# A two-block transformer on one core: depthwise convolutions summed in PSUM, modulation products paced along the feed-forward, merge gates taking turns with taps

## The chip, the cores and the metric

The kernel runs on one core of one Trainium2 chip. The core has five engines that work side by side, each through its own list of instructions in a fixed order: TensorE for matmuls (PE in the profile, PEld its weight loads), VectorE (DVE), ScalarE (ACT), GpSimd (POOL) and SyncE (SP), which here issues every DMA. Matmuls write PSUM, used here as eight banks of [128, 512] float32; everything else lies in SBUF. The metric is the device time of one execution in microseconds.

## The reference

There are 512 tokens of width 1024, all in float32. Block 1 takes a normed input through one wide projection into three branches, and then through a convolutional feed-forward:

```
u = causal_dwconv(h @ w_up, dw_w) + dw_b          # 3 taps a channel
a, v = split(u);  y = (silu(a) * v) @ w_down      # 2 x 2816 channels

a, gate = split(u_conv);  z = a * sigmoid(gate)   # conformer branch, 512 channels
z = causal_dwconv(z, dw_w) + dw_b                 # 31 taps a channel
z = silu(layer_norm(z)) @ w_proj

x = x + (g_a * y_attn + g_b * y_conv) @ w_out     # g = sigmoid(merge gates)
```

`y_attn` is an attention with compressed, selected and windowed keys, 8 heads. Block 2 has two attention layers whose norms are modulated by `mod = silu(c) @ ada_w[layer] + ada_b[layer]`, 3072 numbers for each layer, which depend on the conditioning vector `c` alone.

## The kernel before, in words

Activations lie transposed, features on partitions and the 512 tokens along the free dimension, so that a tile is [128, 512]. A float32 matmul is made of three (`mm3`, L123 to L125): each operand is split into a rounded high part and a low part. So `gemm` of eight K tiles loads weights in two pieces of 512 columns (SP), splits each (ACT at L109, mostly POOL at L110) and runs 24 matmuls into one PSUM bank. That bank is read once by DVE: the evacuation, a multiplication by the row of reciprocal norms (L575 for a merge gate, L666 for an up projection).

The PSUM banks are four pools: `pg` (2) for gemms, `ps` (2) for scores and, from the branches on, for every other gemm (`wide_bank`), `pt` (3) for transposes and `po` (1) for a head's values.

The program is written for a scheduler that orders each engine's list by its own estimate of readiness, with earlier written code first; buffers come from pools in turn. `tc.issue_after(ins)` makes the instructions of a block, as far as they are on `ins`'s engine, stand behind `ins` in that engine's list; it adds no wait, and other engines (the DMAs on SP too) aren't bound by it. What comes out is a fixed list for each engine, with semaphores.

The stages that matter here, with their times in the profile:

- Attention of block 1 (104 to 245 us). For each head and branch: scores (PE, L501), maximum with bias (DVE, L505), exponent (ACT, L507), normalisation (POOL, L509), transposes (PE, L253) split by ACT and DVE (L257, L258), values (PE, L263). `group_compressed` (L448, L449) makes the compressed branch once for each group of four heads. In this stage `conv_input` (L407, L410) makes the four channel tiles `zs` of the conformer branch, and `conv_start` (ACT, L421) the first tap of each.
- Taps and merge gates (to 323 us). A tap is one DVE instruction on a channel tile, `conv[c] = zs[c][:, t:t+512] * w + conv[c]` (L586, 120 of them for 4 tiles), in SBUF. The loop writes both gates of a feature tile and then 16 or 20 taps, for seven of eight tiles. Nothing but data binds them, so the scheduler places taps in attention too.
- The mean over channels (PE, L601 and L602), the squares, a chain of small DVE instructions for the reciprocal root (L156 to L170), its broadcast (PE, L176), norm and SiLU; then the branch projections (`branch`) and the output projection.
- Feed-forward (434 to 814 us). `up(j)`: two gemms, each with its evacuation (L666), first tap (ACT, L668), two taps (DVE, L670), then SiLU and product (POOL, L673). 13 ups, half the down projections, 9 ups, the rest of the down projections. `modulation(n)` is written behind each: a row of 48 columns takes two products with a sum (DVE, L652; operands from HBM, 256 KB each) and an addition of the two sums and the bias (L654). Block 2 needs the results only at its first norm.

Of the kernel before, what the change touches and what calls it, by code (L numbers as in the profile page):

```python
# [43 lines left out]
def build(ctx, tc, I, out):  # L44
# [107 lines left out]
    def newton(x):  # L152
# [4 lines left out]
        # one step of the second order, three eighths of its result, and one of the third:  # L157
        # y * (15 - 10 x y^2 + 3 x^2 y^4) / 8
# [26 lines left out]
    class Squares:  # L185
        """Sums over features of the squares of [128, tokens] chunks."""
# [117 lines left out]
    # compressed keys and values  # L304
# [58 lines left out]
    # keys of the two token branches, queries  # L363
# [37 lines left out]
    # conformer branch: a * sigmoid(gate) = a / 2 * (1 + tanh(gate / 2)), causal depthwise conv, layer norm, silu  # L401
# [16 lines left out]
    def conv_start(c):  # L418
        z = zs[c]
        y = new("h")  # L420
        A.activation(y, z[:, 0:512], AF.Identity, bias=cv("cb", c), scale=cv("cw", c * 31))  # L421
        conv.append(y)

    # queries of one group and its compressed branch
# [67 lines left out]
    # token branches  # L492
# [48 lines left out]
    for h in range(8):  # L541
# [5 lines left out]
        if h == 0:  # L547
            PC.append(group_compressed(0, QG[0]))
            with after():
                conv_start(0)  # L550
# [6 lines left out]
        for b in range(2):  # L557
# [4 lines left out]
            if b == 0 and h in (1, 3, 5):  # L562
                with after():
                    conv_start((h + 1) // 2)
# [5 lines left out]
    def merge_gates(m):  # L570
        gts = []
        for b in range(2):
            ps = gemm(I["w_g"][2 * m + b], xg)
            t = new("m" if m < 4 else "h")
            V.tensor_mul(t, ps, R1)  # L575
            gts.append(t)
        return gts
# [3 lines left out]
    # causal depthwise convolution, layer norm over channels, silu  # L581
    for m in range(7):
        GM.append(merge_gates(m))
        for t in range(1 + 30 * m // 7, 1 + 30 * (m + 1) // 7):
            for c in range(4):
                V.scalar_tensor_tensor(conv[c], zs[c][:, t:t + 512], cv("cw", c * 31 + t), conv[c],  # L586
                                       op0=OP.mult, op1=OP.add)
    # branch projections with their gates, each twice its value
# [25 lines left out]
    GM += [merge_gates(m) for m in range(len(GM), KT)]  # L614
# [8 lines left out]
    # output projection, residual, norm 2  # L623
# [22 lines left out]
    def modulation(n):  # L646
        for l, m in mods[:n]:
            acc = new("s", (128, 16))[:, 0:2]
            for z in range(2):
                raw = new("b") if z else new("z", (128, 542))[:, 0:512]  # L650
                nc.sync.dma_start(raw, I["ada_t"][l, m, :, z * 512:(z + 1) * 512])
                V.tensor_tensor_reduce(out=raw, in0=raw, in1=CA[z], op0=OP.mult, op1=OP.add, scale=1.0,  # L652
                                       scalar=0.0, accum_out=acc[:, z:z + 1])
            V.scalar_tensor_tensor(MD[l][:, m:m + 1], acc[:, 0:1], acc[:, 1:2], cv("adab", 24 * l + m),  # L654
                                   op0=OP.add, op1=OP.add)
        del mods[:n]

    # one pair of up projections with its convolution and product
    def up(j):
        cs = []  # L660
        for b in range(2):
# [4 lines left out]
            V.tensor_mul(u[:, 2:514], ps, R2)  # L666
            t = new("p")
            A.activation(t, u[:, 0:512], AF.Identity, scale=cv("fw", 3 * m), bias=cv("fb", m))  # L668
            for i in (1, 2):
                V.scalar_tensor_tensor(t, u[:, i:i + 512], cv("fw", 3 * m + i), t, op0=OP.mult, op1=OP.add)  # L670
# [11 lines left out]
    for m in range(KT):  # L682
        ps = gemm(I["w_dn"][m][:, 0:11, :], ACTV, 11, wide_bank)
        V.tensor_add(X[m], X[m], ps)
# [4 lines left out]
    # a projection's last chunks go by halves of the tokens, so that the next norm overlaps with it  # L689
# [7 lines left out]
    for m in range(KT):  # L697
# [4 lines left out]
        V.tensor_add(X[m], X[m], ps)  # L702
# [23 lines left out]
    # final norm of block 1 and the first norm of block 2  # L726
    MOD = []
    for l in range(2):
# [533 lines left out]
```

## Time and profile before

| | |
|---|---|
| runs before | 1386.32, 1388.19, 1389.37 us; median 1388.19 |
| profiled execution | its time is told by its span alone: 1387.6 us from the first instruction to the last |
| matmuls, instructions in all | 6337, 19249 |
| mean granted PE clock | 0.971 |
| moved by DMA | 124.74 MB, mean 90 GB/s |

In the page's rows, "x" is a count; in a group of instructions the first number behind the bar is the time in which any of them ran, the second the mean of one in ns, the third the idle time of the engine just before them, with what ended it. A window's row begins with its bounds and length, then busy us (and count) of PE, PEld, DVE, ACT and POOL, the granted PE clock, the busy share of the DMA engines and GB/s. A timeline row begins with start and length in us; equal neighbours are merged, with their count at the end. Rows of one engine overlap a little: the step from one start to the next is shorter than a row's length.

### The profile page before, as it was taken

Reading aid. Unit: us, or ns where it says so; the run is one execution under the profiler, and the core shown is the slowest. Engines: PE = TensorE matmul, PEld = TensorE weight load, DVE = VectorE, ACT = ScalarE, POOL = GpSimd, SP = SyncE. Lnnn points to the kernel's source line nnn. Section 1 sums busy time; section 2 is a strip of 40 time slices with the busy share of each in tenths; the row PEclk is TensorE's granted clock in tenths of the full one; section 3 lists DMA queues with packets and bytes.
Section 4 is the critical chain, followed back from the end, with each engine's and each line's share of the span. In section 5 each row is a group of like instructions: output and inputs, shape, how many; then the busy total and the mean of one; then the engine's idle time right before and its main releaser. Section 6 shows DMA issues by size and latency. Waiting matters only on the chain.

```text
span 1387.6 us, 19249 instructions
## 1 busy us (share of the span) xinstructions
PE 1284.6 (93%) x6337; PEld 1052.3 (76%) x6337; DVE 983.8 (71%) x2117; ACT 690.1 (50%) x1467; POOL 707.2 (51%) x669
## 2 busy tenths in 40 slices
PE   6888889989999998889999997899999989999997
PEld 5777778767877876668888887777777778788886
DVE  7559999984545999972266548967688876666455
ACT  6735467325343323333344434367676745777554
POOL 4248475453643545466555526625444631676642
PEclk9999899999999998999999998999999999999998
DMA  7121101322344777724332320211111120212221
GB/s 222 46 84 56 37 31 56 114 78 82 107 122 129 234 226 228 229 85 137 99 92 78 109 80 26 77 39 35 50 62 39 39 62 28 64 54 62 61 77 61
DMA packets 71971, 124.74 MB, mean 90 GB/s; under 512 B 8256, under 2 KB 17344, under 8 KB 71872
## 3 DMA queue, kind: packets, MB, share of 16 engines
q1 hardware_dynamic: 71872, 123.52, 29.3%
q8 instruction: 50, 0.82, 0.3%
q14 instruction: 49, 0.40, 0.1%
HBM read 121.39 MB, written 2.10 MB: 89 GB/s over the span
## 4 chain that ended last, share of the span: by engine, by line
PE 59%; DVE 28%; ACT 5%; issue 4%; POOL 2%; DMA 2%; SPq 0%; DVEq 0%; ACTq 0%; POOLq 0%
PE pg L123 11%; PE pg L125 10%; PE pg L124 10%; DVE h L586 6%; PE po L263 5%; PE ps L123 4%; PE ps L124 4%; PE ps L125 4%; PE pt L253 3%; DVE p L670 3%; DVE b L652 2%; PE ps L869 2%; DVE z L652 2%; PE ps L1054 2%; PE ps L501 1%
## 5 line engine op out<-in xcount | busy, mean ns | idle before, releaser
L110 POOL TENSOR_TENSOR wl<-wr,wh 128x512 fp32r<-128x512 f32 (+2 forms) x215 | 296.7, 1383 | 319.2 <-ACT wh L109 256.9
L123 PE MATMUL pg<-h,wl 128*128 128x512 f32 x692 | 281.3, 407 | 8.5 <-DVE m L575 5.1
L124 PE MATMUL pg<-h,wh 128*128 128x512 f32 x692 | 277.3, 401 | 0.0
L125 PE MATMUL pg<-h,wh 128*128 128x512 f32 x692 | 276.5, 400 | 0.0
L109 ACT ACTIVATE wh<-wr 128x512 fp32r<-128x512 f32 (+2 forms) x215 | 131.7, 617 | 133.5 <-PE pg L125 74.5
L123 PEld LDWEIGHTS pg<-h,wl 128*128 128x128 f32 x692 | 131.6, 190 | 39.2 <-issue 11.6
L125 PEld LDWEIGHTS pg<-h,wh 128*128 128x128 f32 x692 | 131.6, 190 | 28.3
L124 PEld LDWEIGHTS pg<-h,wh 128*128 128x128 f32 x692 | 131.6, 190 | 27.3 <-issue 0.7
L110 POOL TENSOR_TENSOR m<-t,m 128x512 fp32r<-128x512 f32 (+1 forms) x67 | 93.3, 1392 | 78.7 <-ACT m L109 50.5
L670 DVE SCALAR_TENSOR_TENSOR p<-p,k,p 128x512 f32<-128x512 f32 x88 | 100.4, 1141 | 26.3 <-ACT p L668 25.4
L263 PE MATMUL po<-t,h 128*128 128x512 f32 (+3 forms) x384 | 111.5, 367 | 5.3 <-DVE t L258 2.7
L258 DVE TENSOR_TENSOR t<-pt,t 128x512 fp32r<-128x512 f32 (+1 forms) x160 | 97.3, 629 | 24.9 <-ACT t L257 24.3
L586 DVE SCALAR_TENSOR_TENSOR h<-z,k,h 128x512 f32<-128x512 f32 x120 | 113.4, 988 | 0.1
L257 ACT ACTIVATE t<-pt 128x512 fp32r<-128x512 f32 (+1 forms) x160 | 84.1, 551 | 26.3 <-PE pt L253 25.6
L253 PE MATMUL pt<-k,p 128*128 128x128 f32 x576 | 88.8, 276 | 1.7 <-POOL p L509 0.8
L263 PEld LDWEIGHTS po<-t,h 128*128 128x128 f32 x384 | 67.5, 192 | 27.2 <-ACT t L257 12.0
L253 PEld LDWEIGHTS pt<-k,p 128*128 128x128 f32 x576 | 70.1, 141 | 15.6 <-POOL p L876 3.5
L123 PE MATMUL ps<-h,wl 128*128 128x512 f32 x196 | 78.5, 401 | 1.8 <-ACT h L147 1.6
L124 PE MATMUL ps<-h,wh 128*128 128x512 f32 x196 | 78.0, 398 | 0.3 <-DVE h L148 0.2
L125 PE MATMUL ps<-h,wh 128*128 128x512 f32 x196 | 77.9, 397 | 0.0
L876 POOL TENSOR_SCALAR p<-p,s 128x512 f32<-128x512 f32 x64 | 44.9, 705 | 63.0 <-DVE s L875 62.4
L123 PE MATMUL ps<-h,m 128*128 128x512 f32 (+1 forms) x148 | 59.6, 402 | 15.5 <-DVE p L666 15.4
(367 smaller groups left out, 3003.5 us busy)
## 6 DMA issues: line engine op xcount, KB each, us to landing
b<-ada_t SPq DMA_DIRECT2D x48, 256.0 KB, 3.4
z<-ada_t SPq DMA_DIRECT2D x48, 256.0 KB, 3.4
t<-w_up SPq DMA_DIRECT2D x44, 256.0 KB, 2.9
wr<-w_up SPq DMA_DIRECT2D x44, 256.0 KB, 2.8
wr<-w_g SPq DMA_DIRECT2D x32, 256.0 KB, 2.6
t<-w_dn SPq DMA_DIRECT2D x23, 256.0 KB, 2.7
wr<-w_br SPq DMA_DIRECT2D x16, 256.0 KB, 2.7
wr<-w_gt SPq DMA_DIRECT2D x16, 256.0 KB, 2.7
```

The source lines that it names most:

```text
L109: A.activation(hi[:, :z], raw[:, :z], AF.Copy)
L110: eng.tensor_sub(lo[:, :z], raw[:, :z], f(hi[:, :z]))
L123: PE.matmul(ps, ll, rh, start=start and i == 0, stop=False)
L124: PE.matmul(ps, lh, rl, start=False, stop=False)
L125: PE.matmul(ps, lh, rh, start=False, stop=stop and i == n - 1)
L253: PE.transpose(ps[:, o:o + 128], src, ident)
L257: evac[:] = [A.activation(hi[:, :n], ps[:, :n], AF.Copy)]
L258: evac.append(V.tensor_sub(lo[:, :n], ps[:, :n], f(hi[:, :n])))
L263: PE.matmul(o[:, a:b], v, t[:, pa:pa + b - a], start=start and z == 0, stop=stop and z == 1)
L586: V.scalar_tensor_tensor(conv[c], zs[c][:, t:t + 512], cv("cw", c * 31 + t), conv[c], op0=OP.mult, op1=OP.add)
L652: V.tensor_tensor_reduce(out=raw, in0=raw, in1=CA[z], op0=OP.mult, op1=OP.add, scale=1.0, scalar=0.0, accum_out=acc[:, z:z + 1])
L670: V.scalar_tensor_tensor(t, u[:, i:i + 512], cv("fw", 3 * m + i), t, op0=OP.mult, op1=OP.add)
```

## The change

The convolution sums move to PSUM. A new `acc_bank` gives banks of `pt` and, every fourth time, of `po`. The four conformer sums hold three `pt` banks and the one `po` bank for all their taps; the last tap (t = 30) writes an SBUF tile. In `up`, the first two taps go to such a bank and the third reads it and writes SBUF. `conv_start` leaves the attention loop and is written behind it. Merge gates and taps take turns by single gates: one gate, then 8 or 9 taps that go round the four tiles, 14 times; the gates also use `wide_bank`. The modulation keeps the two sums of each column in a tile `MA` for each layer and adds them, with the bias, in two instructions a layer at the end; its products are put behind the last tap of the up, or the addition of the down projection, that is written before them. The tile `ss` of block 2 moves to another pool; the other lines of the difference are comments.

```diff
+    acount = [0]
+    def acc_bank():
+        acount[0] += 1
+        return new("po" if acount[0] % 4 == 0 else "pt")
...
     def conv_start(c):
-        z = zs[c]
-        y = new("h")
-        A.activation(y, z[:, 0:512], AF.Identity, bias=cv("cb", c), scale=cv("cw", c * 31))
+        y = acc_bank()
+        A.activation(y, zs[c][:, 0:512], AF.Identity, bias=cv("cb", c), scale=cv("cw", c * 31))
         conv.append(y)
+    def conv_tap(c, t):
+        if t == 30:
+            y, conv[c] = conv[c], new("h")
+        else:
+            y = conv[c]
+        return V.scalar_tensor_tensor(conv[c], zs[c][:, t:t + 512], cv("cw", c * 31 + t), y,
+                                      op0=OP.mult, op1=OP.add)
...
-            with after():
-                conv_start(0)
...
-            if b == 0 and h in (1, 3, 5):
-                with after():
-                    conv_start((h + 1) // 2)
...
+    def merge_gate(m, b):
+        ps = gemm(I["w_g"][2 * m + b], xg, bank=wide_bank)
+        t = new("m" if m < 4 else "h")
+        V.tensor_mul(t, ps, R1)
+        return t
+    for c in range(4):
+        conv_start(c)
+    taps = [(c, t) for t in range(1, 31) for c in range(4)]
     for m in range(7):
-        GM.append(merge_gates(m))
-        for t in range(1 + 30 * m // 7, 1 + 30 * (m + 1) // 7):
-            for c in range(4):
-                V.scalar_tensor_tensor(conv[c], zs[c][:, t:t + 512], cv("cw", c * 31 + t), conv[c],
-                                       op0=OP.mult, op1=OP.add)
+        GM.append([])
+        for b in range(2):
+            GM[m].append(merge_gate(m, b))
+            for c, t in taps[len(taps) * (2 * m + b) // 14:len(taps) * (2 * m + b + 1) // 14]:
+                conv_tap(c, t)
...
     def modulation(n):
-        for l, m in mods[:n]:
-            acc = new("s", (128, 16))[:, 0:2]
...
-            V.scalar_tensor_tensor(MD[l][:, m:m + 1], acc[:, 0:1], acc[:, 1:2], cv("adab", 24 * l + m),
-                                   op0=OP.add, op1=OP.add)
+        with tc.issue_after(getattr(paced[0], "ins", paced[0])):
+            for l, m in mods[:n]:
+                for z in range(2):
+                    raw = new("b") if z else new("z", (128, 542))[:, 0:512]
+                    nc.sync.dma_start(raw, I["ada_t"][l, m, :, z * 512:(z + 1) * 512])
+                    V.tensor_tensor_reduce(out=raw, in0=raw, in1=CA[z], op0=OP.mult, op1=OP.add, scale=1.0,
+                                           scalar=0.0, accum_out=MA[l][:, z, m:m + 1])
...
+            a = acc_bank()
             t = new("p")
-            A.activation(t, u[:, 0:512], AF.Identity, scale=cv("fw", 3 * m), bias=cv("fb", m))
-            for i in (1, 2):
-                V.scalar_tensor_tensor(t, u[:, i:i + 512], cv("fw", 3 * m + i), t, op0=OP.mult, op1=OP.add)
+            A.activation(a, u[:, 0:512], AF.Identity, scale=cv("fw", 3 * m), bias=cv("fb", m))
+            for i, dst in ((1, a), (2, t)):
+                paced[0] = V.scalar_tensor_tensor(dst, u[:, i:i + 512], cv("fw", 3 * m + i), a,
+                                                  op0=OP.mult, op1=OP.add)
...
-        V.tensor_add(X[m], X[m], ps)
+        paced[0] = V.tensor_add(X[m], X[m], ps)
...
     for l in range(2):
+        V.tensor_add(MD[l], MA[l][:, 0], MA[l][:, 1])
+        V.tensor_add(MD[l], MD[l], cv("adab", 24 * l, 24))
```

In the changed file the tap is L435, the gate's evacuation L582, the mean L610 and L611, the squares' sums L223 and L224, the broadcast L183, the up's evacuation and taps L675 and L680, the product L663 and DVE's split L152.

Three places of the orders follow. First DVE in attention, where the compressed branch of the second group is made (L410 and L417 are the same evacuation of `conv_input`, L448/L449 and L462/L463 the same sums of the group's scores). Before, with taps on the tiles of channels 0 and 1:

```order
L586 SCALAR_TENSOR_TENSOR h_1071<-z_1009,k_107,h_1071 128x512
L586 SCALAR_TENSOR_TENSOR h_1312<-z_1233,k_107,h_1312 128x512
L586 SCALAR_TENSOR_TENSOR h_1071<-z_1009,k_107,h_1071 128x512
L410 TENSOR_TENSOR p_1719<-pg_1694,r_284 128x512
L448 TENSOR_TENSOR p_1731<-ps_1732,b_1726 128x256
L586 SCALAR_TENSOR_TENSOR h_1312<-z_1233,k_107,h_1312 128x512
L449 TENSOR_TENSOR p_1731<-p_1731,ps_1732 128x256
```

After:

```order
L277 TENSOR_TENSOR h_1073<-po_1528,t_1636 64x512
L414 SCALAR_TENSOR_TENSOR p_1676<-pg_1651,r_284 128x512
L417 TENSOR_TENSOR p_1715<-pg_1690,r_284 128x512
L462 TENSOR_TENSOR p_1727<-ps_1728,b_1722 128x256
L463 TENSOR_TENSOR p_1727<-p_1727,ps_1728 128x256
L462 TENSOR_TENSOR p_1727<-ps_1739,b_1722 128x256
```

The taps that stood between have left this place, as they have the whole of attention.

Second, DVE and PE from the end of attention to the mean. DVE before, where seven taps stand between the evacuations of two gates:

```order
L575 TENSOR_TENSOR m_2841<-pg_2816,r_284 128x512
L586 SCALAR_TENSOR_TENSOR h_1839<-z_1722,k_107,h_1839 128x512
L586 SCALAR_TENSOR_TENSOR h_2229<-z_2150,k_107,h_2229 128x512
L586 SCALAR_TENSOR_TENSOR h_1839<-z_1722,k_107,h_1839 128x512
L586 SCALAR_TENSOR_TENSOR h_2229<-z_2150,k_107,h_2229 128x512
L586 SCALAR_TENSOR_TENSOR h_1839<-z_1722,k_107,h_1839 128x512
L586 SCALAR_TENSOR_TENSOR h_2229<-z_2150,k_107,h_2229 128x512
L586 SCALAR_TENSOR_TENSOR h_1071<-z_1009,k_107,h_1071 128x512
L575 TENSOR_TENSOR m_2880<-pg_2855,r_284 128x512
```

After, where attention's last instructions (L277 adds a head's halves) meet the first taps:

```order
L152 TENSOR_TENSOR h_2687<-h_1073,h_2686 128x512
L435 SCALAR_TENSOR_TENSOR pt_2702<-z_1009,k_107,pt_2702 128x512
L152 TENSOR_TENSOR h_2691<-h_1488,h_2690 128x512
L435 SCALAR_TENSOR_TENSOR pt_2704<-z_1231,k_107,pt_2704 128x512
L277 TENSOR_TENSOR h_2311<-po_2614,t_2683 64x512
L152 TENSOR_TENSOR h_2695<-h_1914,h_2694 128x512
L582 TENSOR_TENSOR m_2747<-ps_2722,r_284 128x512
L152 TENSOR_TENSOR h_2699<-h_2311,h_2698 128x512
L435 SCALAR_TENSOR_TENSOR pt_2706<-z_1718,k_107,pt_2706 128x512
L435 SCALAR_TENSOR_TENSOR po_2708<-z_2144,k_107,po_2708 128x512
L435 SCALAR_TENSOR_TENSOR pt_2702<-z_1009,k_107,pt_2702 128x512
L435 SCALAR_TENSOR_TENSOR pt_2704<-z_1231,k_107,pt_2704 128x512
```

All 120 taps now stand from here on, with 8 or 9 of them between two evacuations, each on the next of the four banks. PE at the mean, before (`pg` of a merge gate behind it, and 18 more of its matmuls ahead of the squares' sums):

```order
L124 MATMUL pg_3329<-h_181,wh_3324 128x512
L125 MATMUL pg_3329<-h_180,wh_3324 128x512
L601 MATMUL ps_3379<-z_3376,k_119 128x512
L602 MATMUL ps_3379<-h_2229,k_119 128x512
L123 MATMUL pg_3461<-h_121,wl_3451 128x512
```

After (ahead of it the first half-length branch gemm, behind it the sums and the broadcast at once):

```order
L123 MATMUL pg_3559<-h_2698,wl_3554 128x512
L124 MATMUL pg_3559<-h_2699,wh_3553 128x512
L125 MATMUL pg_3559<-h_2698,wh_3553 128x512
L610 MATMUL ps_3383<-z_3380,k_119 128x512
L611 MATMUL ps_3383<-h_3378,k_119 128x512
L223 MATMUL ps_3401<-k_119,z_3395 128x1
L224 MATMUL ps_3401<-k_119,p_3398 128x1
```

The merge gate that stood behind the mean now stands ahead of it, and the next gate follows behind the broadcast.

Third, DVE in the second pair of ups. Before (the rows named ISA are products and the reading of their sums):

```order
L670 SCALAR_TENSOR_TENSOR p_4382<-p_4379,k_107,p_4382 128x512
L654 SCALAR_TENSOR_TENSOR k_4290<-s_4706,k_107 128x1
L670 SCALAR_TENSOR_TENSOR p_4382<-p_4379,k_107,p_4382 128x512
L652 ISA z_4715,s_4714<-z_4715,z_4292 128x512
L652 ISA s_4714 128x1
L652 ISA b_4718,s_4714<-b_4718,z_4295 128x512
L652 ISA s_4714 128x1
L652 ISA z_4817,s_4816<-z_4817,z_4292 128x512
L652 ISA s_4816 128x1
L145 TENSOR_TENSOR h_4389<-p_4338,h_4388 128x512
L666 TENSOR_TENSOR p_4437<-ps_4412,r_4288 128x512
L654 SCALAR_TENSOR_TENSOR k_4290<-s_4714,k_107 128x1
```

After:

```order
L680 SCALAR_TENSOR_TENSOR pt_4446<-p_4443,k_107,pt_4446 128x512
L680 SCALAR_TENSOR_TENSOR p_4447<-p_4443,k_107,pt_4446 128x512
L674 MEMSET p_4488 128x2
L675 TENSOR_TENSOR p_4488<-pg_4463,r_4292 128x512
L680 SCALAR_TENSOR_TENSOR po_4491<-p_4488,k_107,po_4491 128x512
L680 SCALAR_TENSOR_TENSOR p_4492<-p_4488,k_107,po_4491 128x512
L663 ISA z_4502,k_4296<-z_4502,z_4298 128x512
L663 ISA k_4296 128x1
L663 ISA b_4505,k_4296<-b_4505,z_4301 128x512
L663 ISA k_4296 128x1
L663 ISA z_4508,k_4296<-z_4508,z_4298 128x512
L663 ISA k_4296 128x1
```

The products that stood between the two taps of an up and ahead of the next evacuation (L666) now stand behind both ups' taps.

More of the change, by code (lines that the diff above doesn't have):

```diff
@@ L568, in build @@
         OS = [split(t) for t in OF]
-    def merge_gates(m):
-        gts = []
-        for b in range(2):
[L573 to L577, printed above, removed]
-    GM = []
-    for m in range(7):
-        GM.append(merge_gates(m))
-        for t in range(1 + 30 * m // 7, 1 + 30 * (m + 1) // 7):
-            for c in range(4):
-                V.scalar_tensor_tensor(conv[c], zs[c][:, t:t + 512], cv("cw", c * 31 + t), conv[c],
-                                       op0=OP.mult, op1=OP.add)
+    def merge_gate(m, b):
[3 more added lines that the diff above has]
+        return t
+    GM = []
+    for c in range(4):
+        conv_start(c)
+    taps = [(c, t) for t in range(1, 31) for c in range(4)]
+    for m in range(7):
+        GM.append([])
+        for b in range(2):
+            GM[m].append(merge_gate(m, b))
+            for c, t in taps[len(taps) * (2 * m + b) // 14:len(taps) * (2 * m + b + 1) // 14]:
+                conv_tap(c, t)
     def branch(b, m, src):
@@ L612, in build @@
         ZS.append(split(conv[c]))
-    GM += [merge_gates(m) for m in range(len(GM), KT)]
+    GM += [[merge_gate(m, b) for b in range(2)] for m in range(len(GM), KT)]
     MG = []
@@ L638, in build @@
     MD = [new("k", (128, 24), tag=f"md{l}") for l in range(2)]
+    MA = [new("k", (128, 2, 24), tag=f"ma{l}") for l in range(2)]
+    paced = [None]
     CA = []
@@ L646, in modulation @@
     def modulation(n):
-        for l, m in mods[:n]:
-            acc = new("s", (128, 16))[:, 0:2]
[L649 to L654, printed above, removed]
-                                   op0=OP.add, op1=OP.add)
+        with tc.issue_after(getattr(paced[0], "ins", paced[0])):
[5 more added lines that the diff above has]
+                                           scalar=0.0, accum_out=MA[l][:, z, m:m + 1])
         del mods[:n]
@@ L701, in build @@
         ps = gemm(I["w_dn"][m][:, 11:18, :], ACTV[11:], 7, wide_bank)
-        V.tensor_add(X[m], X[m], ps)
+        paced[0] = V.tensor_add(X[m], X[m], ps)
         modulation(1)
@@ L787, in build @@
     VA, QN, KN, CN, KR = [], [], [], [], []
-    ss = new("s", (128, 40), tag="ss")
+    ss = new("k", (128, 40), tag="ss")
     def key_values(i):
```

## The prediction

> **What bounds the kernel now.** I read the page first (busy shares, the 40 slices, the chain), then the stages by time window, then who ends the waits, and last single rows.
>
> ```profile
> PE 1284.6 (93%) x6337; PEld 1052.3 (76%) x6337; DVE 983.8 (71%) x2117; ACT 690.1 (50%) x1467; POOL 707.2 (51%) x669
> PE   6888889989999998889999997899999989999997
> DVE  7559999984545999972266548967688876666455
> PE 59%; DVE 28%; ACT 5%; issue 4%; POOL 2%; DMA 2%; SPq 0%; DVEq 0%; ACTq 0%; POOLq 0%
> ```
>
> PE is busy 93% of the span and dips where DVE stands at 9: slices 4 to 8 (attention and the convolution taps) and 13 to 17 (first half of the feed-forward). Those are the stages that the change edits. By window, with busy us of each engine and the granted clock:
>
> ```profile
> 104.00:244.50 140.50, 128.42 (x675) 104.92 (x673) 133.44 (x335) 85.02 (x216) 94.06 (x102) 0.95 0.14 44
> 244.50:322.60 78.10, 70.13 (x287) 54.63 (x288) 64.25 (x72) 22.11 (x38) 37.49 (x24) 0.98 0.32 98
> 322.60:433.50 110.90, 108.23 (x463) 85.53 (x462) 56.34 (x79) 49.08 (x80) 54.81 (x40) 0.98 0.34 103
> 451.00:613.50 162.50, 143.51 (x578) 113.01 (x577) 156.60 (x324) 54.58 (x88) 85.91 (x58) 0.95 0.68 208
> 680.00:760.00 80.00, 80.00 (x349) 65.13 (x348) 47.82 (x62) 33.63 (x54) 45.49 (x34) 1.00 0.32 90
> 1180.00:1340.00 160.00, 159.10 (x822) 129.98 (x821) 95.03 (x309) 104.46 (x264) 102.11 (x127) 1.00 0.22 67
> ```
>
> The windows are attention; merge gates with the remaining taps; branches and output projection; the first 24 up gemms after a slow start; later up gemms; and, for comparison, the windowed attention of block 2. The fifth is the pace that PE can hold: 349 matmuls in 80 us, so 0.23 us each, and 5.5 us a gemm of 24. The fourth holds 24 gemms, 576 matmuls worth 132.5 us, in 162.5 us: 30 us lost, of which PE idle is 162.5 - 143.5 = 19.0 and the clock (0.95, so 5%) 8. Attention loses 140.5 - 128.4 = 12.1 idle and 7.0 of clock; the gate stage 8.0 and 1.6. After a long idle of PE its clock is halved for some microseconds, so the clock terms go with the idle terms: behind the 3.60 us below, a matmul takes 0.63 that at full clock takes 0.40.
>
> ```profile
> by line: DVE h L586 21.5%; PE po L263 13.6%; PE ps L501 11.8%; PE pt L253 9.1%; PE pg L123 6.6%; PE pg L125 6.3%; PE pg L124 6.3%; DVE p L505 3.7%; issue 3.3%; DVE h L226 2.4%; PE po L524 2.3%; DVE t L258 2.2%; DVE p L410 1.3%; ACT p L507 1
> 154.79 9.04 DVE h L586 x8
> 243.75 0.73 PE L524 MATMUL po<-h,k 32*128 32x512 f32 x2
> PE ps L501 <- DVE s L505: 6.8, 5, 3.1
> PE ps L501 <- DVE p L449: 3.6, 1, 3.6
> PE pg L123 <- DVE m L575: 5.1, 3, 2.1
> PE ps L123 <- DVE p L666: 15.4, 6, 3.6
> 600.80 0.52 PE L123 MATMUL ps<-h,m 128*128 128x512 f32 x1 [3.60 <-DVE p L666]
> 601.12 0.63 PE L124 MATMUL ps<-h,m 128*128 128x512 f32 x1
> 680.13 0.40 PE L123 MATMUL pg<-h,m 128*128 128x512 f32 x1
> ```
>
> The first row is the chain of waits in the attention window: its largest member is the taps (L586). One piece of it, eight taps in 9.04 us at 154.79, stands ahead of the L449 for which PE then waits 3.6 us. L524 at 243.75 is the last head's. The two waits for L575 and L666 are those of the gate stage and the feed-forward: a bank that a late DVE has not read.
>
> **The change, part by part.** Prices first:
>
> ```profile
> L586 DVE SCALAR_TENSOR_TENSOR h<-z,k,h 128x512 f32<-128x512 f32 x120 | 113.4, 988 | 0.1
> L586 DVE SCALAR_TENSOR_TENSOR h<-z,k,h 128x512 f32<-128x512 f32 x64 | 59.0, 947 | 0.1
> 205.87 0.73 DVE L586 SCALAR_TENSOR_TENSOR h<-z,k,h 128x512 f32<-128x512 f32 x1
> 234.33 1.39 DVE L586 SCALAR_TENSOR_TENSOR h<-z,k,h 128x512 f32<-128x512 f32 x2
> 262.26 4.15 DVE L586 SCALAR_TENSOR_TENSOR h<-z,k,h 128x512 f32<-128x512 f32 x3
> 262.27 3.59 POOL L110 TENSOR_TENSOR wl<-wr,wh 128x512 fp32r<-128x512 f32 x2 [3.74 <-ACT wh L109]
> 324.56 2.48 DVE L605 SCALAR_TENSOR_TENSOR h<-ps,h 128x512 f32<-128x512 f32 x4 [1.03 <-PE ps L602]
> 334.54 2.50 DVE L610 TENSOR_TENSOR h<-h,r 128x512 f32<-128x512 f32 x4
> ```
>
> A tap alone takes 0.73 and two take 1.39, so a free tap comes every 0.66 us. Three taps under two of POOL's TENSOR_TENSORs take 4.15: with two SBUF operands a tap waits for POOL, and its mean price is 113.4 / 120 = 0.945. A scalar-tensor-tensor that reads PSUM (L605, four in 2.48) has the pitch of one that reads SBUF alone (L610, four in 2.50). No row shows DVE writing PSUM. Bounds for the new tap: 0.60, the pitch of those two, and 0.945, no gain. I take 0.66, the free tap, because a tap with its sum in PSUM has one SBUF tensor left and nothing to wait for; 0.29 us less each. [...]
>
> *Attention.* 64 taps (59.0 us) leave a DVE that was busy 133.4 of 140.5 us. [...] I let three quarters of the 19.1 us come back, 14.3; both ends stay open, none and all. 21 gate matmuls (28 instead of 49, counted in the orders) also move behind the stage, 4.8 us. So it ends at 244.5 - 19.1 = 225.4, between 220.6 and 239.7.
>
> *Taps and gates.* All 120 taps now stand behind attention, since their four banks are the transposes' and the values'. Queue on DVE from there: 120 x 0.66 = 79.2, fourteen gate evacuations at 0.60 = 8.4, four splits 2.4, one head's sum 0.6, the two sums for the mean 1.9: 92.5 us. PE has 344 matmuls for it, 79 us: here DVE becomes the bound, with 6.3 us from one evacuation to the next (8.6 taps) against a gemm's 5.5. The mean's matmul (L601, now L610) comes at 225.4 + 92.5 = 317.9; it was 322.6. Behind it PE has 396 matmuls instead of 432, but none between the mean and the row of reciprocal roots:
>
> ```profile
> 322.64 1.02 PE L601 MATMUL ps<-z,k 128*128 128x512 f32 x2
> 327.75 0.69 DVE L202 TENSOR_TENSOR z<-z,p 128x512 f32<-128x512 f32 x1
> 330.75 0.16 DVE L170 TENSOR_SCALAR s<-ps 128x4 f32<-128x4 f32 x1 [2.31 <-PE ps L217]
> 333.82 0.69 DVE L182 COPY r<-ps 128x512 f32<-128x512 f32 x1 [1.25 <-PE ps L176]
> ```
>
> From L601 to the broadcast, whose end releases the copy at 333.8, are some 10.7 us, in which PE ran 27 matmuls (6.2 us); now it idles there, and a halved clock behind it costs, as an estimate from the 1.6 us of the second window, some 1.7. The third window lost 2.7 us idle and 2.2 of clock; I leave that. So 10.7 + 396 x 0.23 + 1.7 + 4.9 = 108.4 us to the feed-forward: 426.3 instead of 433.6. This half of the change brings 7.3 us, between 12.1 and -7.0 by attention's end, and 4 us less for each 0.033 on a tap.
>
> *Feed-forward.*
>
> ```profile
> L670 DVE SCALAR_TENSOR_TENSOR p<-p,k,p 128x512 f32<-128x512 f32 x44 | 48.8, 1109 | 2.5 <-ACT p L668 2.4
> L652 DVE CUSTOM_DVE_ANT_0 b<-b,z 128x512 f32<-128x512 f32 x44 | 43.6, 990 | 1.2 <-DMA b<-ada_t 1.2
> L652 DVE CUSTOM_DVE_ANT_0 z<-z,z 128x512 f32<-128x512 f32 x44 | 36.4, 828 | 0.0
> L654 DVE SCALAR_TENSOR_TENSOR k<-s,k 128x1 f32<-128x1 f32 x44 | 18.3, 417 | 0.0
> L666 DVE TENSOR_TENSOR p<-ps,r 128x512 f32<-128x512 f32 x11 | 7.5, 680 | 0.0
> 694.53 2.45 DVE L670 SCALAR_TENSOR_TENSOR p<-p,k,p 128x512 f32<-128x512 f32 x2 [0.88 <-ACT p L668]
> ```
>
> In the 162.5 us DVE does 44 of the 48 modulation columns: 43.6 + 36.4 + 18.3 = 98.3 us, ahead of what PE waits for. Now they follow the taps of their up, 1.5 columns a pair instead of 3.7, and the 48 L654 (0.42 each) become four small sums. A pair of ups on DVE: two evacuations 1.3, two waits for ACT of 0.9 to 1.3, which products no longer fill, four taps at 0.66 to 0.79 = 2.9, one split 0.7, and 1.5 columns of two products at 0.83 to 0.99 = 2.7: 9.4 to 10.2 us against PE's 11.0. PE is the bound again, by a little, and four banks cover a late pair. Of the 30 us I take 28. What was 60% busy in the later ups gets the other columns at the same pace: nothing, covered by the slack of DVE there (47.8 of 80). The weights on SP's queue now stand behind product loads that wait for a product; they are issued some five gemms ahead, 27 us, which covers that. Four sums of 24 columns at the end: nothing, under the last down gemms.
>
> Sum: 7.3 + 28 = 35.3 us off the profiled execution, whose span of 1387.6 is 0.6 below the median of 1388.2: 1352.3, and 1353 by the median.
>
> **Rivals.** (a) Attention keeps its length: ACT and POOL, at 85 and 94 of 140 us in chains of score, exponent and product, hold PE where taps did; its idle rows name L505, which itself waits little. Then -7.0 + 28: 1367. Against it stand the eight taps ahead of L449. (b) The products in DVE's fixed order behind taps that wait for ACT hold the next evacuation; the pair above has 0.8 us to spare, and a two-column pair none. Half of 28 is lost: 1367. (c) The other side: a PSUM-to-PSUM tap is no cheaper than 0.945. Then the queue behind attention is 34 us longer, and the feed-forward, at 11 us a pair, gives 20: 7.3 - 34 + 20 = -7, so 1395. The sign turns at a tap of some 0.9. (d) A tap into PSUM must wait for the one before to end. The later L670 price that: 2.45 for two, the second stretched by POOL, the first 0.79 to its successor. At 0.79, 120 x 0.13 = 15.6 us are lost: 1368. [...]
>
> **How the numbers follow.** Chances: the forecast, 1353, 0.50, in its own range 1343 to 1362; (a) 0.17, (b) 0.13, (d) 0.10, (c) 0.06, better than 1343 0.04. The range is 1338 to 1376: it takes in (a), (b) and (d), and leaves out (c) and the tails. A change within 0.2% (2.8 us) is about what a measurement of this kernel cannot tell from none: 0.03. Slower is (c) and a little of (a) and (b) together, 0.07; faster is the rest, 0.90.
>
> **What would show it.** Right: no PE wait over 1 us in attention but at its first group; taps 0.74 long without rows of 1.8; 92 us from the last head to the mean; a PE idle of some 4 us and then 2 us around the mean's roots; up gemms every 5.5 us from the third on, with the clock at 1.00. Wrong: taps over 0.8 us apart; an attention stage that still ends near 240; ups with idle before L123 released by the evacuation.

## The result: 1356.9 us, 31 us less

The changed kernel takes 1356.88 us in the median of four runs (1354.97 to 1359.69), the kernel before 1387.86 beside it; the ratio put on record is 0.9784, with a 95% interval from 0.9769 to 0.9799 (that of the two medians alone is 0.9777). The forecast was 1353 us, in a range from 1338 to 1376. The profiled execution is the longest of the four (1359.69 us, span 1357.9), so the stages are compared span against span: 1387.6 to 1357.9, 29.7 us less, where the sum had 35.3.

The profile after, from its page (busy shares, PE and its clock in 40 slices):

```profile
PE 1278.4 (94%) x6337; PEld 1050.7 (77%) x6337; DVE 945.6 (70%) x2073; ACT 689.9 (51%) x1467; POOL 686.2 (51%) x669
PE   7889999996999999999999989899999989999997
PEclk9899999995999999999999998899999989999998
```

The long dips of PE in attention and in the first ups are gone. One slice is left, the tenth, with PE at 6 and its clock at 5. By window (columns as before):

```profile
104.00:224.90 120.90, 119.77 (x657) 97.44 (x656) 79.91 (x270) 80.73 (x210) 74.38 (x100) 1.00 0.16 51
224.90:317.50 92.60, 82.38 (x345) 65.63 (x344) 92.37 (x140) 29.01 (x49) 37.55 (x29) 0.95 0.30 96
317.50:431.20 113.70, 105.65 (x426) 83.20 (x426) 54.38 (x77) 46.09 (x75) 49.76 (x36) 0.90 0.29 90
440.70:579.20 138.50, 138.50 (x601) 112.74 (x600) 106.57 (x182) 60.73 (x99) 85.29 (x61) 1.00 0.50 157
739.97:782.32 42.35, 39.88 (x169) 31.48 (x168) 31.55 (x52) 13.06 (x24) 26.11 (x19) 1.00 0.67 211
```

They are attention, which ends 19.6 us earlier and now idles PE for 1.1 us; the gates with all 120 taps, where DVE is busy for 92.4 of 92.6 us; the stretch from the mean to the first up, whose clock is 0.90; the 25 gemms up to the first down projection, with PE busy in every microsecond at full clock; and the second down projection, which took 39.35 us before:

```profile
774.31:813.66 39.35, 39.35 (x169) 31.64 (x168) 13.72 (x17) 13.85 (x25) 20.79 (x17) 1.00 0.48 143
```

The same places as a ledger, in us from the start of the span:

| | before | forecast | after | gained so far |
|---|---|---|---|---|
| last head's values end | 244.5 | 225.4 | 224.9 | 19.6 |
| mean's matmul | 322.6 | 317.9 | 317.5 | 5.1 |
| first up gemm | 433.6 | 426.3 | 431.2 | 2.3 |
| first down gemm | 613.6 | | 579.2 | 34.3 |
| second down, first gemm | 774.3 | | 740.0 | 34.3 |
| second down, end | 813.7 | | 782.3 | 31.3 |
| end | 1387.6 | 1352.3 | 1357.9 | 29.7 |

So two places lost what the sum had not: the chain behind the mean, 5 us, and the second down projection, 3 us. The last 1.7 us are lost in pieces below 0.7 us in block 2; they weren't followed further.

**The chain behind the mean.** PE's clock in three stretches, and PE's rows in it:

```profile
303.00:316.00 13.00, 4.38 (x12) 3.21 (x12) 13.00 (x20) 2.06 (x4) 2.53 (x2) 0.72 0.13 41
316.00:336.00 20.00, 12.53 (x36) 9.16 (x37) 9.74 (x23) 5.31 (x8) 0.00 (x0) 0.50 0.05 14
336.00:340.00 4.00, 4.00 (x18) 3.17 (x18) 2.24 (x4) 3.93 (x7) 0.51 (x1) 0.99 0.00 0
```
```profile
317.53 2.07 PE L610 MATMUL ps<-z,k 128*128 128x512 f32 x2 [3.86 <-DVE z L209]
319.39 1.92 PE L611 MATMUL ps<-h,k 128*128 128x512 f32 x2
325.28 0.59 PE L223 MATMUL ps<-k,z 128*128 128x1 f32 x2 [3.97 <-DVE z L209]
...
330.83 2.07 PE L183 MATMUL ps<-k,s 128*128 128x128 f32 x8 [1.98 <-DVE s L172]
332.55 0.77 PE L123 MATMUL ps<-h,wl 128*128 128x512 f32 x1
```

For 20 us the granted clock is 0.50. In the chain PE waits for DVE three times, 3.86, 3.97 and 1.98 us, and between the waits it has only the chain's own few matmuls. They run at half clock as well: two of the mean's matmuls take 2.07 us against 1.02 before (the row of L601 at 322.64, quoted ahead). From the mean to the end of the broadcast it is 15.0 us; in the kernel before 10.9, with gate matmuls in every gap. The trace shows what follows for a chain: with idles of 3.86 and 3.97 us ahead of it and within it, this one stayed at half clock for its whole length. In e11_all4 below the clock is halved behind a shorter idle, of 2.11 us.

**The second down projection.** Two of PE's rows there, and pieces of the chain of waits up to 772 us:

```profile
760.67 0.50 PE L123 MATMUL ps<-h,wl 128*128 128x512 f32 x1 [0.86 <-POOL wl L110]
767.47 0.50 PE L123 MATMUL pg<-h,wl 128*128 128x512 f32 x1 [1.61 <-POOL wl L110]
```
```profile
748.06 2.94 DMA z<-ada_t
...
755.02 0.60 DVE b L663
...
755.66 0.33 SPq L662
...
756.04 5.68 DMA t<-w_dn
...
761.74 0.64 ACT h L109
...
762.45 1.30 POOL h L110
```

PE waits for weights. A product load (L662) can be issued only when the product that read its buffer is done (DVE, 755.02 to 755.62); it stands in SP's queue ahead of the load of `w_dn`, which goes out 0.4 us behind it and lands late for the splits on ACT and POOL. From 742 to 766 us SP waits six times for such a product, 8.0 us in all. The transfers are also slower here: the 256 KB loads of `w_dn` into `t` land after 3.9 us in the median, 2.8 in the kernel before, with the DMA engines busy for 0.67 of the time instead of 0.48. How much of the 3 us is owed to the hold in the queue and how much to the slower landing isn't shown.

### The profile page after: what moved, and what is told of

The parts are those of the page before. It is cut to its first block, busy times and chain, and to the rows that moved or that the text cites. A ratio compares the mean times of both kernels' runs of the same rounds, so it can differ in the third digit from the quotient of the medians.

```text
span 1357.9 us, 19273 instructions
## 1 busy us (share of the span) xinstructions
PE 1278.4 (94%) x6337; PEld 1050.7 (77%) x6337; DVE 945.6 (70%) x2073; ACT 689.9 (51%) x1467; POOL 686.2 (51%) x669
## 5 line engine op out<-in xcount | busy, mean ns | idle before, releaser
L110 POOL TENSOR_TENSOR wl<-wr,wh 128x512 fp32r<-128x512 f32 (+2 forms) x215 | 285.7, 1330 | 344.2 <-ACT wh L109 282.9
L123 PE MATMUL pg<-h,wl 128*128 128x512 f32 x628 | 252.8, 403 | 8.0 <-DVE h L582 6.4
L125 PE MATMUL pg<-h,wh 128*128 128x512 f32 x628 | 250.6, 399 | 0.0
L124 PE MATMUL pg<-h,wh 128*128 128x512 f32 x628 | 250.6, 399 | 0.0
L109 ACT ACTIVATE wh<-wr 128x512 fp32r<-128x512 f32 (+2 forms) x215 | 132.8, 618 | 182.4 <-PE pg L125 95.7
L123 PEld LDWEIGHTS pg<-h,wl 128*128 128x128 f32 x628 | 118.8, 189 | 33.0 <-issue 6.8
L125 PEld LDWEIGHTS pg<-h,wh 128*128 128x128 f32 x628 | 119.0, 190 | 26.5 <-issue 0.7
L124 PEld LDWEIGHTS pg<-h,wh 128*128 128x128 f32 x628 | 119.1, 190 | 24.9 <-issue 0.4
L110 POOL TENSOR_TENSOR m<-t,m 128x512 fp32r<-128x512 f32 (+1 forms) x67 | 88.5, 1320 | 74.3 <-ACT m L109 68.4
L123 PE MATMUL ps<-h,wl 128*128 128x512 f32 x260 | 105.4, 405 | 2.6 <-ACT h L154 1.6
L124 PE MATMUL ps<-h,wh 128*128 128x512 f32 x260 | 104.6, 402 | 0.4 <-DVE h L155 0.2
L125 PE MATMUL ps<-h,wh 128*128 128x512 f32 x260 | 104.0, 400 | 0.0
L663 DVE CUSTOM_DVE_ANT_0 b<-b,z 128x512 f32<-128x512 f32 x48 | 73.6, 1533 | 1.6 <-DMA b<-ada_t 1.6
L109 ACT ACTIVATE m<-t 128x512 fp32r<-128x512 f32 (+2 forms) x78 | 47.0, 604 | 41.1 <-PE ps L123 12.7
L123 PE MATMUL pg<-h,m 128*128 128x512 f32 (+1 forms) x144 | 57.2, 398 | 6.5 <-DVE m L110 6.5
```

Source lines behind the costliest of these rows:

```text
L109: A.activation(hi[:, :z], raw[:, :z], AF.Copy)
L110: eng.tensor_sub(lo[:, :z], raw[:, :z], f(hi[:, :z]))
L123: PE.matmul(ps, ll, rh, start=start and i == 0, stop=False)
L124: PE.matmul(ps, lh, rl, start=False, stop=False)
L125: PE.matmul(ps, lh, rh, start=False, stop=stop and i == n - 1)
```

## Experiments

Each kernel is the changed one with the edit shown, unless said otherwise; times are medians, ratios are to the kernel before on the same chip, with 95% intervals.

| kernel | us (lowest to highest) | ratio |
|---|---|---|
| e1_ffn_only | 1361.8 (1360.4 to 1362.4) | 0.9814 [0.9789, 0.9838] |
| e2_conv_only | 1385.5 (1383.9 to 1388.5) | 0.9983 [0.9970, 0.9996] |
| e3_conv_sbuf | 1385.7 (1383.7 to 1389.5) | 0.9985 [0.9967, 1.0002] |
| e4_ffn_sbuf | 1378.0 (1377.4 to 1379.1) | 0.9933 [0.9909, 0.9957] |
| e5_unpaced | 1377.6 (1372.8 to 1378.8) | 0.9915 [0.9893, 0.9937] |
| e6_cols_early | 1359.9 (1359.2 to 1360.6) | 0.9796 [0.9780, 0.9813] |
| e7_early4 | 1349.6 (1348.2 to 1350.3) | 0.9719 [0.9704, 0.9733] |
| e9_warm | 1352.2 (1348.5 to 1352.8) | 0.9733 [0.9715, 0.9751] |
| e10_cols_done | 1358.5 (1357.4 to 1360.4) | 0.9785 [0.9763, 0.9808] |
| e11_all4 | 1350.2 (1347.7 to 1356.1) | 0.9719 [0.9689, 0.9748] |
| e11_all8 | 1345.2 (1340.6 to 1345.6) | 0.9681 [0.9655, 0.9707] |
| e12_cols_down | 1340.4 (1339.3 to 1342.7) | 0.9662 [0.9644, 0.9679] |

### The two halves, each alone

```diff
 # e1: conv_start, merge_gates and the taps' loop of the kernel before
 # e2: up()'s taps and modulation() of the kernel before
```

> The feed-forward half of the change alone: PSUM sums and paced products in the feed-forward, attention, gates and convolution as before. Theory (the halves add up): attention still ends at 244 and the mean comes at 322.6, the up gemms run every 5.54 us, so some 30 us off the 24 of them and up to 2 us at the norm ahead, less the 3 us that the changed kernel loses at 760: 1361 us, 1358 to 1364. Rival (the feed-forward gained because the convolution no longer ran into it): the up gemms keep some of their waits, 1370 or more.

> The convolution half alone: taps in PSUM behind attention and gates in turn, the feed-forward as before. Theory: attention ends at 225, the mean comes at 317.5, the granted clock is 0.50 for some 20 us around it, the first up gemm starts 2 us earlier than before, and the feed-forward loses its 30 us: 1385 us, 1383 to 1387. Rival (the term of 7.3 us was right and the changed kernel lost it further on, at its first ups): 1380.5.

Both came as the first theory said, 1361.8 and 1385.5: the halves add up to the whole (27 and 3 us below the kernel before beside them, of 31 in all), and the convolution half brings the feed-forward little although attention gives back 19.6 us. In e2 the mean's matmul is at 317.9 and the wait of 3.97 us ahead of L223 is there too, so the chain's loss belongs to that half alone.

### The convolution's sums in SBUF, in the same order

```diff
-        y = acc_bank()
+        y = new("h")
...
-    for c in range(4): conv_start(c)
+    for c in range(4):
+        with after(): conv_start(c)
...
     # conv_tap, at t == 30
-            y, conv[c] = conv[c], new("h")
+            y = conv[c]
```

> The changed kernel with the convolution's sums in SBUF, at the same place in DVE's order (behind attention, with the same taps between the same gates). Theory (the tap's price is POOL's hold on it): attention still ends at 225, taps under a POOL TENSOR_TENSOR take 1.8 us, 120 taps cost 0.95 us in the mean instead of 0.74, so the mean comes 25 to 28 us later: 1383 us, 1378 to 1388. Rival (the order brought it, not PSUM): 1357, within 3 us.

1385.7: PSUM brought it. The taps' groups, first of the changed kernel, then of e3:

```profile
L435 DVE SCALAR_TENSOR_TENSOR pt<-z,k,pt 128x512 f32<-128x512 f32 x86 | 59.7, 741 | 0.0
```
```profile
L435 DVE SCALAR_TENSOR_TENSOR h<-z,k,h 128x512 f32<-128x512 f32 x120 | 109.2, 979 | 0.1
```

A tap takes 741 ns with its sum in PSUM, 979 with both operands in SBUF: 0.24 us by 120 is 28.6 us, and the mean came at 345.4 instead of 317.5, 27.9 later. That an SBUF tap pays for POOL's work beside it shows in the kernel before: the 61 of its 120 taps that run beside a POOL TENSOR_TENSOR take 1.21 us in the mean and up to 1.80, the other 59 take 0.75.

### The feed-forward's two parts

```diff
 # e4: up(), sums in SBUF, products still paced
-            a = acc_bank()
-            t = new("p")
+            a = t = new("p")
 # e5: modulation(), products in the scheduler's order, sums in PSUM
-        with tc.issue_after(getattr(paced[0], "ins", paced[0])):
+        if True:
```

> The changed kernel with the feed-forward's sums in SBUF, the products still paced behind the taps. Theory (the pacing carries the feed-forward's gain): four taps of a pair cost some 0.35 us more each, 1.4 us on the 8.5 us that DVE is busy of 11.1, PE stays the bound: 1357 us, 1355 to 1360. Rival (the PSUM sum carries it): a pair of two columns takes 11.5 us or more, 24 up gemms and 18 later ones lose 10 us or more: 1367 or more.

> The changed kernel with PSUM sums everywhere, the products in the planner's own order again (28 columns' products ahead of the first up's evacuation, then some 3 columns a pair). Theory (both parts are needed, since DVE's load in the first 24 ups must fit into 11.1 us a pair): three or four columns a pair at 2.3 us make 15 us a pair, less 1.5 us for the cheaper taps, so ups lose 12 to 25 us, the second down gains its 3 us back: 1370 us, 1363 to 1380. Rival (the PSUM taps alone make room, as SBUF sums alone cost 21 us in the run before): 1355, 1352 to 1360.

Here e4's theory fell, and its rival held: with paced products and SBUF sums it is 1378.0, not 1357. With PSUM sums and products unpaced (e5) it is 1377.6, in the range of its theory. With the convolution half in place throughout, neither part is 1385.5 (e2), either alone about 7.5 less, both 1356.9, 28.6 less. The estimate for e4 took 0.35 us for a tap's gain and left out how POOL's instructions fall. The group of taps of e4 from 460 to 570 us, and its rows of two pairs of ups, the first with two columns, the second with one:

```profile
L679 DVE SCALAR_TENSOR_TENSOR p<-p,k,p 128x512 f32<-128x512 f32 x33 | 44.3, 1342 | 18.1 <-ACT p L677 17.5
```
```profile
504.00 0.68 DVE L675 TENSOR_TENSOR p<-ps,r 128x512 f32<-128x512 f32 x1
505.57 2.46 DVE L679 SCALAR_TENSOR_TENSOR p<-p,k,p 128x512 f32<-128x512 f32 x2 [0.88 <-ACT p L677]
...
509.96 2.94 DVE L679 SCALAR_TENSOR_TENSOR p<-p,k,p 128x512 f32<-128x512 f32 x2 [1.32 <-ACT p L677]
...
518.05 0.68 DVE L675 TENSOR_TENSOR p<-ps,r 128x512 f32<-128x512 f32 x1
530.00 0.68 DVE L675 TENSOR_TENSOR p<-ps,r 128x512 f32<-128x512 f32 x1
```

A tap takes 1342 ns there and the pairs 14.05 and 11.95 us from evacuation to evacuation, against PE's 11.1: DVE falls behind for good. The changed kernel's group and rows at the same place:

```profile
L680 DVE SCALAR_TENSOR_TENSOR pt<-p,k,pt 128x512 f32<-128x512 f32 x15 | 11.3, 756 | 14.9 <-ACT pt L678 14.9
```
```profile
500.63 0.76 DVE L680 SCALAR_TENSOR_TENSOR pt<-p,k,pt 128x512 f32<-128x512 f32 x1 [0.85 <-ACT pt L678]
501.42 0.75 DVE L680 SCALAR_TENSOR_TENSOR p<-p,k,pt 128x512 f32<-128x512 f32 x1
...
511.30 0.68 DVE L675 TENSOR_TENSOR p<-ps,r 128x512 f32<-128x512 f32 x1
521.24 0.68 DVE L675 TENSOR_TENSOR p<-ps,r 128x512 f32<-128x512 f32 x1
```

Where e4 loses its 21 us is telling: 6 in the ups, 3 in the first down, and 12 in the second down, where PE idles for 11.7 us, waiting for the splits of its weights. Late taps make late products, and the weights come late; whether late products in SP's queue hold them, or the splits that stand behind late work in the lists of ACT and POOL, wasn't separated. In e5, where the products of the first columns stand ahead of the first up's evacuation again, the norm ahead of the feed-forward waits 10 us, and the second down has no wait at all.

### PE's clock around the mean

```diff
+    warm(mp, 20)                     # matmuls into the mean's bank, ahead of it
...
+    with tc.issue_after(mean): warm(st, 14)
...
+    with tc.issue_after(total.end): warm(bc, 6)
```

The extra matmuls are overwritten by the first real one in each bank; the operand of all three groups is a copy of a late tap, so that they can't run early.

> The changed kernel with 40 more matmuls whose results are overwritten: 20 into the mean's bank ahead of the mean, 14 ahead of the sums, 6 ahead of the broadcast, where PE idles. Theory (the idles halve PE's clock, and the halved clock lengthens the chain itself): granted clock 1.00 from 317 to 336, the chain from the mean's matmul to the broadcast 11 us instead of 15, the 36 matmuls behind it 8.4 us instead of 10.1: 1352 us, 1350 to 1354. Rival (the clock there is low for another reason, or the extra matmuls delay the chain by what they save): 1357 or more.

1352.2, 4.7 us less, with the window of e9 that answers to the second of the three above:

```profile
316.00:336.00 20.00, 20.00 (x97) 16.07 (x96) 11.18 (x24) 9.20 (x14) 1.27 (x1) 1.00 0.04 14
```

The mean's matmul comes 0.8 us later there (318.4), the broadcast's end 3.1 earlier (329.4), so the chain takes 11.0 us. Forty useless matmuls make the kernel faster: it was the clock.

### Sixteen taps in attention

```diff
+    EARLY = 4
     def conv_start(c):
-        y = acc_bank()
+        y = new("h")                 # called in the attention loop again
...
+        if t == EARLY + 1:
+            conv[c] = acc_bank()
```

> The changed kernel with the first four taps of each channel (16 of 120) summed in SBUF during attention, and the other 104 in PSUM behind it. Theory (the mean is set by DVE's queue behind attention): the queue gets 10.5 us shorter, attention 0 to 4 us longer (64 taps cost it some 15), PE's idle of 6.4 us ahead of the mean goes: the mean 7 to 10 us earlier, 1349 us, 1346 to 1352. [...]

1349.6, as the theory said, though the mean comes 6.7 us earlier, not 7 to 10, and PE still waits 2.1 and 1.5 us ahead of it. Attention and the stage behind it in e7:

```profile
93.36:225.90 132.54, 127.22 (x683) 102.64 (x683) 100.44 (x308) 85.68 (x220) 83.65 (x104) 0.99 0.15 49
225.90:310.90 85.00, 81.42 (x341) 64.64 (x339) 82.03 (x124) 26.58 (x45) 37.43 (x29) 0.98 0.33 102
```

From the first score to the last values it takes 2.3 us more than in the changed kernel, from there to the mean 7.4 us less, and the chain runs at a clock of 0.69 instead of 0.50.

### Where the second down's weights are held

```diff
 # columns:      first down, a gemm   later ups, a pair    second down
-# changed       1                    1 or 2 by turns      7
+# e6            1 or 2 by turns      2                    none
+# e10           2                    2, done by the 7th   none
+# e12           2 or 3 by turns      1 or 2, done by 6th  none
```

> The changed kernel with no product behind the second down: its 7 columns go to the first down (4) and the later ups (3 of their 4 odd pairs), 2 columns a pair there. Theory (SP's queue: product loads that wait for a product hold the loads of w_dn): no PE wait above 0.5 us at the second down, its eight gemms take 39.4 us as before instead of 42.4, and two columns a pair still fit: 1353.9 us, 1352.5 to 1355.5. Rival (the weights come late for another reason there, or two columns a pair don't fit in 11.1 us): 1357 or more.

> The changed kernel with all columns done three pairs before the last up: 2 a gemm in the first down (16), 2 a pair in the first six later ups, 1 in the seventh, none behind. The run before only moved products to the last ups, and PE's waits for w_dn came earlier and grew. Theory (a product load waits in SP's queue for the product two before it, with the loads of w_dn behind it): with no product load among the loads of w_dn these come in time, the eight gemms of the second down take 39.4 us without a wait: 1354 us, 1352.5 to 1356. Rival (POOL or the DMA rate sets the second down's weights, whoever shares the queue): waits of 2 us or more stay, 1357 or more.

Both missed, 1359.9 and 1358.5, on the numbers that their rivals named; neither can be told from the changed kernel, whose interval they overlap. Without a product behind the second down, its waits came earlier and grew. In e10 it begins at 740.51:

```profile
753.52 0.79 PE L123 MATMUL ps<-h,wl 128*128 128x512 f32 x1 [2.76 <-POOL wl L110]
```

Set beside each other load by load, the SP rows show where the time goes. In the kernel before, one load of `w_dn` goes out 11.2 us ahead of the second down's first gemm; in the changed kernel the same one 13.2 us ahead; in e10 7.7. The lag builds up over the pairs with two columns; SP's rows of e10 in one of them:

```profile
706.53 0.33 SPq L662 DMA_DIRECT2D z<-ada_t  x1
708.84 0.33 SPq L662 DMA_DIRECT2D b<-ada_t  x1
709.26 0.38 SPq L108 DMA_DIRECT2D wr<-w_up  x1
```

A weight load goes out 0.42 us behind a product load that was itself held, 31.2 us ahead of that gemm against 34.4 in the changed kernel. The lag is 3.2 us there and 5.5 at the load above, and the product loads don't account for all of it: the last of them goes out at 717.97, and over the 99.7 us ahead of the second down SP waits for products for 18.6 us, in the changed kernel for 17.1. From 718 on the loads of `w_dn` wait for POOL's splits, up to 5.9 us. This stands ahead of one such split:

```profile
739.53 1.28 POOL L684 TENSOR_TENSOR p<-p,p 128x512 f32<-128x512 f32 x1 [1.18 <-DVE p L674]
740.84 0.63 ACT L151 ACTIVATE h<-p 128x512 fp32r<-128x512 f32 x1 [2.97 <-POOL p L684]
741.38 0.61 ACT L109 ACTIVATE wh<-t 128x512 fp32r<-128x512 f32 x1
742.13 1.30 POOL L110 TENSOR_TENSOR wl<-t,wh 128x512 fp32r<-128x512 f32 x1 [1.32 <-ACT wh L109]
743.45 0.33 SPq L108 DMA_DIRECT2D t<-w_dn  x1
```

POOL's product of the up (L684) waits for DVE, whose last tap of that up ends at 739.45, and ACT's split of it (L151) waits for POOL; the split of the weights (L109, L110) stands behind both in their lists, and the next load of `w_dn` waits for its buffer. The pairs with two columns take DVE 12.0 to 12.2 us (evacuations at 684.66, 696.72, 708.75, 720.80 and 733.05), more than PE's 11.1, so DVE falls behind there, as in e4. So there are two ways in which columns that are too dense make the weights late, SP's queue and the lists of ACT and POOL. The last run thins them out to 1.5 a pair; its base is the kernel with 32 taps in attention (next), which has e10's columns.

> The kernel with 32 taps in attention, its columns put elsewhere: 2.5 a gemm in the first down (20), 1.5 a pair in the first six later ups, none behind (it had 2, 2 and none). Theory (the loads of the weights lag where product loads of two columns a pair, 16 product loads in four pairs, hold SP's queue; 1.5 a pair let the stream keep its lead in the changed kernel): the loads of w_dn are back at 11 us ahead of the second down instead of 7.7, its waits of 2.8 and 0.9 us and 6 us of lost time go to under 1: 1341 us, 1338 to 1343. Rival (the second down's weights are late without any product load near them, or the first down can't take 2.5 columns in 7.6 us): 1345 or more.

1340.4, in the range of its theory. The load is back at 11.7 us ahead, and the windows of the second down, first with the columns of e10 (e11_all8), then of e12:

```profile
721.59:765.90 44.31, 40.45 (x170) 31.37 (x169) 16.00 (x22) 15.62 (x28) 22.65 (x19) 1.00 0.44 131
```
```profile
726.28:765.64 39.36, 39.36 (x170) 31.64 (x168) 13.14 (x17) 13.30 (x24) 21.11 (x17) 1.00 0.47 141
```

The second down takes 4.95 us less, without a wait, and the medians differ by as much, though the intervals of the two kernels overlap a little. With 1.5 columns a pair both DVE's lag and SP's queue get lighter, so e12 shows that the density of the columns is the cause, and not which of the two ways carried it in e10.

### All of it together

```diff
 # e7's edit (EARLY = 4 or 8), e10's columns, and warm(mp, 6), warm(st, 14), warm(bc, 6)
```

> Sixteen taps in attention (1349.6 in the run before), the columns done early, and 26 overwritten matmuls around the mean (6, 14 and 6) together. Theory (three separate places: DVE's queue, PE's clock in the chain, SP's queue): 1349.6 - 3 for the second down - 3.5 for the chain at full clock: 1343 us, 1341 to 1346. Rival (they share: with fewer taps behind attention the clock is lost for a shorter time, so the extra matmuls bring nothing): 1346 or more.

> The same with eight taps of each channel, 32 of 120, in attention. Theory: behind attention DVE's queue is another 10.5 us shorter and PE becomes the bound there with 345 matmuls, 79.5 us; attention 1 to 4 us longer; of the 3 us that PE still waits ahead of the mean 2 or 3 go, so 1341 to 1345 us, near the kernel with 16. Rival (attention was free for 16 taps only because they were few: DVE and POOL collide): 1347 or more.

With 16 taps the rival held: 1350.2, no better than e7 alone. Its profiled execution is the slowest of its four, the others being 1347.7 to 1352.1. Its second down has e10's waits, and PE still idles 2.1 us shortly ahead of the mean and 1.4 at it; the clock in the chain is 0.78 in spite of the extra matmuls, and the chain takes 13.2 us as in e7. The clock there falls behind shorter idles than those above, in two windows of e11_all4:

```profile
304.50:307.90 3.40, 1.29 (x6) 0.82 (x5) 2.09 (x4) 2.15 (x4) 1.26 (x1) 1.00 0.31 81
308.00:311.30 3.30, 3.30 (x9) 2.57 (x8) 2.44 (x4) 0.00 (x0) 0.00 (x0) 0.51 0.21 74
```

Behind a single idle of 2.11 us the clock is halved for some 3.3 us. It is halved again from 321.7 to 328.3 us, behind idles of 1.38 and 0.76 us and a dozen matmuls of one column each. So idles as long as the 3.86 and 3.97 us above aren't needed for it; what exactly sets it off these runs don't show.

With 32 taps PE no longer waits there: 1345.2, just above its range (1341 to 1345), though the profiled execution is the fastest of the four, at 1340.6. So in its other runs PE may wait there more than this profile shows. The mean of e11_all8 and the chain behind it:

```profile
292.00:305.70 13.70, 13.09 (x57) 10.03 (x55) 12.26 (x17) 4.71 (x8) 5.19 (x4) 1.00 0.28 80
305.70:316.60 10.90, 10.90 (x56) 8.45 (x56) 5.24 (x15) 3.81 (x6) 1.27 (x1) 1.00 0.14 44
```

How much of e12's 16.5 us below the changed kernel is owed to its 26 extra matmuls alone was not tried.

## Why the prediction was right, and where its sum was off

- **The tap, 0.66 us.** Right: three in 2.06 us, 0.658 from start to start, with the sum read from PSUM and written there:

```profile
230.84 2.06 DVE L435 SCALAR_TENSOR_TENSOR pt<-z,k,pt 128x512 f32<-128x512 f32 x3
```

Rival (c) needed 0.945; e3 shows that price where the sum stays in SBUF.
- **A tap behind the one it reads.** Rival (d)'s 0.79 is real where a tap reads the sum of the one just before it (500.63 to 501.42 above). The convolution goes round four banks and doesn't pay it.
- **Attention's end, 225.4.** Measured 224.9. "Three quarters come back" was the author's estimate between none and all, which no run had shown, and low: PE idles for 1.1 us there, of 12.1, at a clock of 1.00. So the hit within 0.5 us is in part luck. Rival (a) is out.
- **The mean, 317.9.** Measured 317.5; DVE's queue of 92.5 us took 92.6.
- **From the mean to the feed-forward, 108.4 us.** This term was mis-sized: it took 113.7, and the first up came at 431.2 instead of 426.3. The prediction named PE's idling there and priced a halved clock behind the chain (1.7 us, and the 36 matmuls did take 10.1 us against 8.4). It kept the chain itself at 10.7 us (10.9 by its own rows), from a kernel in which PE was busy in the gaps; at half clock it took 15.0. e9 shows that the clock is the cause. Of the 5.3 us that the stretch took beyond the sum that is 4.3; the remaining 1.0 comes from 396 matmuls at 0.2335 us instead of the rounded 0.23, 1.4 us, less some smaller idles.
- **Feed-forward, 28 of 30 us.** From the first up to the first down 148.0 us instead of 180.0, so 32 came back: 29.5 of the 30, and 2.5 at the norm that its first gemm overlaps, which the sum had not counted. But the pair was worked out too low, at 9.4 to 10.2 us with 1.5 columns. A pair with two takes DVE 12.2 us from evacuation to evacuation (499.10 to 511.30), one with one 9.9 (511.30 to 521.24): 11.07 in the mean, PE's own pace, and from 455 to 580 us DVE waited for PE for only 0.2 us. The term that was mis-sized is the products, priced at 0.99 and 0.83 us. After the change, from 446 to 579 us, they take:

```profile
L663 DVE CUSTOM_DVE_ANT_0 b<-b,z 128x512 f32<-128x512 f32 x18 | 31.6, 1757 | 0.0
L663 DVE CUSTOM_DVE_ANT_0 z<-z,z 128x512 f32<-128x512 f32 x18 | 17.9, 995 | 0.0
```

That is 1.4 us a pair more than the sum had. The 0.8 us that it left to spare weren't there; that DVE's mean came out at PE's pace and not above it, while the banks cover each two-column pair, is luck. Rival (b) is out, though its "a two-column pair none" was right, and e4 and e5 show that 28.6 us need both parts.
- **"Issued some five gemms ahead, which covers that."** This step failed: with product loads among the loads of `w_dn` in SP's queue, the second down lost 3.0 us. In e12, on another base, the columns are placed otherwise and it has no wait. The later ups did cost nothing: 99.7 us before and after.
- Together: 35.3 - 5 (chain) + 4 (feed-forward) - 3 (second down) - 1.7 (block 2) = 29.6, and 29.7 were measured. The 4 us that the feed-forward gave beyond its 28 cover part of the other three, so the time is nearer to the forecast than its terms are.

## What to carry to other kernels

When work that filled PE's gaps is moved away, price the short dependent chain that it covered at PE's halved clock, for its whole length (here 15.0 us instead of 10.9), or leave it some filler (11.0 us in e9). When an engine that just fits its partner's pace also releases buffers, follow the buffers: what is late next may be a load that stands behind another in a queue, or a split that stands behind late work in another engine's list. And two edits that each bring 7 us may bring 29 together, since what counts is whether the engine's load gets below its partner's pace.

## What the runs showed of the hardware

The half clock lasted for 20 us in which PE was busy for 12.5, in pieces between waits of 2 to 4 us; in e11_all4 it came behind an idle of 2.1 us as well. In the kernel before, the granted clock was 0.50 at the end of each of the eight idles of PE of 3.08 to 5.70 us or 1.2 us after it at the latest, for 3.4 to 10.2 us; of the shorter ones, that of 1.63 us at 390.14 had a half clock behind it, and that of 2.84 us at 565.70 had none. A tap with its sum in PSUM doesn't feel POOL: 74 of the 120 run beside a POOL TENSOR_TENSOR and take 0.742 us in the median, the other 46 take 0.740. The products, with two SBUF operands, do: the 15 that meet no such instruction take 0.68 to 0.69 us, the 81 that meet one up to 1.78.
